# Evicting and scattering an expert's down product behind the branch for long lists, in a mixture-of-experts stage on one core

## The chip, the cores and the metric

One core of a Trainium2 chip runs the whole program: TensorE (PE; its weight loads are shown as PEld), VectorE (DVE), ScalarE (ACT), GpSimd (POOL) and SyncE (SP), with 16 DMA engines. The metric is the device time of one execution in microseconds (us); a smaller time is better.

## The reference

Two blocks follow each other on 512 tokens of width 1024, in float32. The first is a state-space and convolution mixer with an MLP, the second a Fourier and gated-delta mixer followed by the mixture of experts that this case is about:

```python
def moe_ffn(h, w_group, b_group, w_router, b_router, w_gate, w_up, w_down):
    """Hierarchical MoE: top-1 expert group, then top-2 SwiGLU experts within that group."""
...
    def expert_block(args):
        xb, e = args
        hid = jax.nn.silu(xb @ w_gate[e]) * (xb @ w_up[e])
        return hid @ w_down[e]

    ys = lax.map(expert_block, (xs, blk_expert)).reshape(n_slots, d)
    out = jnp.zeros((n + 1, d), ys.dtype).at[slot_tok].add(ys * slot_w[:, None].astype(ys.dtype))
...
    x = x + mod_x[5] * moe_ffn(modulate(rmsnorm_2(x, norm2_g), mod_x[3], mod_x[4]), ...)
...
    return rmsnorm_2(x, final_g)
```

There are 32 experts (4 groups of 8). `w_gate` and `w_up` of one expert are 1024 x 512, `w_down` is 512 x 1024: 6 MB of float32 for each expert. Each token goes to two experts, so 1024 rows are spread over 32 lists whose lengths depend on the data.

## The kernel before, in words

The stage is the function `moe`. It takes the experts one after another, 32 iterations `i`, in 16 pairs `p` (`h` is 0 for the first of a pair, 1 for the second). The first 64 tokens of each list are always computed; what a list holds beyond that is computed behind branches whose condition `nx` (the list's extra blocks of 32 tokens) is read from memory into a register of each engine.

- **Weights.** `load(i)` issues six transfers of 1 MB on SP's queue (L1652) into a ring of 15 chunks. A chunk's next transfer waits until PE has read the chunk for the last time. The up and gate chunks of expert i are read by `gate_up` and by the branch of iteration i, the down chunks in iteration i+1.
- **One iteration on PE**, whose order is written out by hand (`tc.manual_schedule` for PE alone; the order on the other engines is chosen by a planner): `gate_up` (L1733, 32 instructions, in its middle `hide`, the transposes of the previous expert's hidden rows, L1748, copied out by ACT in L1751); for h = 1 `columns` (L1719, 1722), the next pair's tokens turned over; then `finish(i - 1)`, the down product of the previous expert into the PSUM tile `dn` (L1760, 16 instructions); then the branch `longer(i)` (L1900); then small one-hot products (`per_slot`, L1669), for h = 1 after the transposes of `prepare` (L1814).
- **Evict and scatter.** `finish` also holds the eviction of the product by DVE (L1764, in `outputs`), into one of two buffers `y`, and its scatter by POOL to the rows of `yd` in memory (L1703): two rows for each token, one for each of its experts. Both stand ahead of the branch. For the last pair (p = 15) there is no scatter: the rows are split into two parts (L1774, L1775) and placed by one-hot products at the very end (`combined`, L1786, L1787).
- **The branch.** `tc.If(nx > 0, label=...)` at L1900 is entered for a list over 64, an inner `tc.If(nx > 1)` at L1901 for one over 96. A list with one extra block runs `block_up` (L1829) and `block_down` (L1847) in the inner `Else`; a longer one runs `block_up`, `wide_up`, `block_down` and `wide_down` in the inner `If`. `block_down` scatters its product. `wide_down` does not: it splits it and adds it to the accumulator `acc` in SBUF with eight one-hot products (L1786) and eight DVE additions (L1787). The tile `dn` (one buffer) holds the down product of `finish` and also the products of `block_up` and `block_down`.
- **The hint.** In `gate_up` PE is told after its first matmul where the outer branch will jump (`mark_branch_hint_location`). There is no hint for the inner branch, nor on another engine.
- **The end.** In iteration 31 `fetch_back` reads `yd` back in four transfers (L1947), `read_back` adds them to `acc` (L1952, eight DVE additions of 128 x 1024). Two of the four tiles are added with high priority ahead of a branch over all engines (`tc.If(some > 0)`, L2021), the other two at the end. Then come the last expert's product, the one-hot products of the last pair, a norm and the output.

Of the kernel before, what the change touches and what calls it, by code (L numbers as in the profile page):

```python
# [84 lines left out]
class Kern:  # L85
# [1526 lines left out]
    def moe(self, out):  # L1612
# [15 lines left out]
        def t_(tag, shape, dt=F32, bufs=1, pool=mp):  # L1628
            return pool.tile(shape, dt, tag=tag, bufs=bufs, name=self.nm(tag))

        def p_(tag, bufs):
            return pp.tile([P, 512], F32, tag=tag, bufs=bufs, name=self.nm(tag))
# [118 lines left out]
                put(hT[:, q:q + 2], pt[:, 64 * q:64 * q + 128].rearrange("p (k s) -> p k s", k=2))  # L1751
            return hT

        def outputs(ws, hT, wsl):


            dn = p_("dn", 1)
            for q in range(4):
                for j in range(2):
                    M.matmul(dn[64 * j:64 * j + 64], hT[:, q], ws[4 + q // 2][:, q % 2, 512 * j:512 * j + 512],  # L1760
                             start=(q == 0), stop=(q == 3), tile_position=(0, 64 * j), skip_group_check=True)
            self.turn = 4 - self.turn
            y = r1[:, self.turn]
            V.scalar_tensor_tensor(y, dn, wsl, m5, op0=ALU.mult, op1=ALU.mult)  # L1764
            return y

        def down(ws, hT, wsl, idf, yy, tag=""):


            y = outputs(ws, hT, wsl)  # L1770
# [49 lines left out]
            V.tensor_tensor(xb, xb, self.gs[:, 1].unsqueeze(2).broadcast_to(S_), op=ALU.add)  # L1820
            return xb

        def block_up(ws, xb, h):

            gu = p_("dn", 1)
            for k in range(8):
                for o in range(4):
                    j, c = divmod(o, 2)
                    M.matmul(gu[32 * o:32 * o + 32, :256], xb[:, k, 32 * h:32 * h + 32],  # L1829
                             ws[2 * (k // 4) + j][:, k % 4, 256 * c:256 * c + 256],  # L1830
                             start=(k == 0), stop=(k == 7), tile_position=(0, 32 * o), skip_group_check=True)
            sb, hb = (t_(n, [P, 256])[:64] for n in ("sb", "hb"))
            A.activation(sb, gu[64:, :256], AF.Silu)
            V.tensor_mul(hb, gu[:64, :256], sb)
            return hb

        def block_down(ws, w, hb, h, sx):

            pt = p_("tr", 1)
            for c in range(2):  # L1840
                M.transpose(pt[:, c * 64:c * 64 + 64], hb[:, c * P:c * P + P], self.ident[:64, :64])
            hT = t_("hTb", [P, 4, 32])
            V.tensor_copy(hT.rearrange("p (c h) s -> p h c s", h=2), pt[:, :P].rearrange("p (h c s) -> p h c s", h=2, c=2))
            dn = p_("dn", 1)
            for q in range(4):
                for o in range(4):
                    M.matmul(dn[32 * o:32 * o + 32, :256], hT[:, q], ws[4 + q // 2][:, q % 2, 256 * o:256 * o + 256],  # L1847
                             start=(q == 0), stop=(q == 3), tile_position=(0, 32 * o), skip_group_check=True)
            yb = t_("sb", [P, 256])
            V.scalar_tensor_tensor(yb, dn[:, :256], w[:, 1:2], m5b, op0=ALU.mult, op1=ALU.mult)  # L1850
            if sx is not None:
                scatter(sx, yb, 4)
                return
            yH = t_("hb", [P, 256], F32R)
            A.copy(yH, yb)
# [29 lines left out]
        def wide_up(ws):  # L1885
            return gate_up(ws, normed(prepare(64), t_("xb2", [P, 512]).rearrange("p (k s) -> p k s", k=8)), 0, None, "cb", 3)

        def wide_down(ws, w, gh):
            for fn in combined([down(ws, hidden(gh), w[:, 1:2], w[:, 0:1], yx, "b")]):
                fn()  # L1890

        def length(i, **kw):
# [1 line left out]
            return nc.values_load(self.extra[0:1, e:e + 1], min_val=0, max_val=14, **kw)  # L1894

        def longer(i, ws, nx, first, xb, far, label=None):
            w, sx = first[0], first[2]
            if sx is not None:
                sx = sx[:, i % 2:i % 2 + 1]
            with tc.If(nx > 0, label=label):  # L1900
                with tc.If(nx > 1) as more_:  # L1901
                    hb = block_up(ws, xb, i % 2)
                    g = wide_up(ws)
                    block_down(ws, w[:, i % 2], hb, i % 2, sx)
                    wide_down(ws, far[1][:, i % 2], g)
                    with ExitStack() as ies:
                        for b in range(1, INLINE):
                            ies.enter_context(tc.If(nx > 1 + 2 * b))
                            far = further(per_slot(places(ranks(i // 2), 96 + 64 * b, 64, "b"), vals(i // 2)))
                            rows2(far, i % 2)  # L1910
                            wide_down(ws, far[1][:, i % 2], wide_up(ws))
                with more_.Else():
                    block_down(ws, w[:, i % 2], block_up(ws, xb, i % 2), i % 2, sx)

        engs = [mybir.EngineType.PE, mybir.EngineType.DVE, mybir.EngineType.Activation, mybir.EngineType.Pool]
        mes = ExitStack()
# [59 lines left out]

            held["hT"] = hidden(gh, A.copy)

        def finish(i, ws):

            p, h = divmod(i, 2)
            w, sx = wv[p]
            if p < 15:
                scatter(sx[:, h:h + 1], outputs(ws, held["hT"], w[:, h, 1:2]), 2)
            else:
                pair.append(down(ws, held["hT"], w[:, h, 1:2], w[:, h, 0:1], yr[:, h]))

        before = None
        for i in range(32):
            p, h = divmod(i, 2)  # L1990
            if h == 0 and p < 14:
                oh = onehot(p + 2)
            ws = load(i)
            if i == 31:
                for t in range(3):
                    fetch_back(t)
                with tc.high_priority():
                    for t in range(2):
                        read_back(t)
            if h == 0 and 0 < p < 15:  # L2000
                oh1 = places(ranks(p + 1), 64, 32, "1")
            if i:
                with tc.If(length(i, engines=[mybir.EngineType.Pool]) > 1):
                    rows2(far, h)
            if h and p < 15:
                oh2 = places(ranks(p + 1), 96, 64, "2")
            gate_up(ws, xs, 64 * h, gh, between=[hide] if i else [ahead], start=4 if i else 1, label=f"long{i}")
            if i == 0:
                with tc.If(length(0, engines=[mybir.EngineType.Pool]) > 1):
                    rows2(far, 0)  # L2010
                xb = normed(prepare(0), xb1)
                oh1 = places(ranks(1), 64, 32, "1")
            if h and p < 15:
                columns()
            if i:
                finish(i - 1, before)
            nx0, nx = nx, length(i + 1, engines=engs) if i < 31 else None
            if i < 31:
                longer(i, ws, nx0, firsts[p], xb, far, f"long{i}")
            else:  # L2020
                with tc.If(some > 0, label="long31"):  # L2021
                    longer(i, ws, nx0, firsts[p], xb, far)
                    with tc.If(most > 1 + 2 * INLINE):
                        longest()
                fetch_back(3)
            if h and p < 15:
                ps = prepare(0)
                if p < 14:
                    wv.append(fetch(per_slot(oh, vals(p + 2))))
                xb = normed(ps, xb1)  # L2030
                far = further(per_slot(oh2, vals(p + 1)))
            if h == 0 and p < 15:
                firsts.append(more(p + 1, per_slot(oh1, vals(p + 1))))
            if i == 29:
# [5 lines left out]
        finish(31, before)  # L2040
        ob = t_("oh2", [P, T], F32R)
        V.tensor_scalar(ob, iota, firsts[15][1], None, op0=ALU.is_equal)
        pair.append((ob, yyb))
        for t in range(2, 4):
            read_back(t)
        mes.close()

# [67 lines left out]
```

## Time and profile before

| | |
|---|---|
| three runs: median, lowest to highest | 2015.5 us, 2010.29 to 2017.15 us |
| the profiled execution: its own time, its span | 2006.19 us, 2004.4 us |
| mean granted clock of TensorE in it | 0.929 of full speed |
| busy share of the span: PE, DVE, ACT, POOL | 88%, 56%, 29%, 16% |
| expert stage: first gate_up matmul, last product out of it | 1428.8 us, 1983 us |

The span runs from the first to the last instruction; positions in the rows below are us from its start. In this execution four lists are over 64 tokens and one of them is over 96: L1829 ran 256 times, which is 4 times 64, and `gate_up` into `cb` (the wide one) once. Engine names with a q (DVEq, PEq) mean the engine's sequencer, which here is where a branch is passed and signalled.

### The profile page before, as it was taken

To read this page: it belongs to the slowest core of one execution; us is meant where nothing else is said; L and a number is where in the kernel's file an instruction comes from. 1 tells how busy PE (TensorE), PEld (TensorE's weight loads), DVE (VectorE), ACT (ScalarE), POOL (GpSimd) and SP (SyncE) were. 2 spreads that over 40 slices of the span, in tenths; PEclk is the share of its full clock that TensorE was granted. 3 is DMA by queue.
4 is the path that set the end of the run, shared out by engine and by line. 5 is a ranking of instruction groups with operands and counts; after the bars stand their busy time and mean duration, and the time that the engine had idled before them with its cause. 6 is when DMAs were issued, how large, how long until landed. Compare 5 with 4: busy or idle time off the path is not lost. (4 is left out here: it accounts for less than half of the span.)

```text
span 2004.4 us, 24512 instructions
## 1 busy us (share of the span) xinstructions
PE 1767.2 (88%) x9177; PEld 1149.3 (57%) x9177; DVE 1118.7 (56%) x2240; ACT 586.8 (29%) x991; POOL 318.5 (16%) x209
## 2 busy tenths in 40 slices
PE   6778889699999999999988988999598888888984
PEld 4545556376786787777765666887333333333331
DVE  4799898833543665584457698573532223233225
ACT  3122323232433254332335533332411111111112
POOL 0334444421000000000012122003011111101010
PEclk9878889799999999999998898999699989989998
DMA  5111111138556332221222111015799999979994
GB/s 141 57 63 42 45 61 64 42 133 293 184 183 238 106 117 94 85 84 64 84 84 81 47 43 56 12 54 207 290 365 413 412 364 387 367 280 374 415 412 164
DMA packets 150196, 351.07 MB, mean 175 GB/s; under 512 B 20407, under 2 KB 107008, under 8 KB 130155
## 3 DMA queue, kind: packets, MB, share of 16 engines
q1 hardware_dynamic: 135533, 302.52, 40.9%
q0 software_dynamic: 8928, 33.37, 4.6%
q10 hardware_dynamic: 5534, 12.54, 1.7%
q8 instruction: 121, 1.98, 0.4%
q14 instruction: 80, 0.66, 0.1%
HBM read 339.63 MB, written 18.89 MB: 179 GB/s over the span
## 5 line engine op out<-in xcount | busy, mean ns | idle before, releaser
L125 ACT CAST wh<-w 128x1024 fp32r<-128x1024 f32 (+1 forms) x184 | 179.4, 975 | 407.2 <-PE acc L131 339.8
L126 POOL TENSOR_TENSOR wl<-w,wh 128x1024 fp32r<-128x1024 f32 (+1 forms) x76 | 182.8, 2409 | 623.5 <-PE acc L138 372.7
L1733 PE MATMUL gu<-ew,moe 128*64 128x512 f32 x1024 | 259.0, 640 | 9.5 <-issue 5.7
L126 DVE TENSOR_TENSOR wl<-w,wh 128x1024 fp32r<-128x1024 f32 (+1 forms) x108 | 123.2, 1141 | 119.2 <-PE acc L138 88.6
L1733 PEld LDWEIGHTS gu<-ew,moe 128*64 128x64 f32 x1024 | 75.6, 145 | 139.5 <-issue 128.9
L130 PE MATMUL acc<-xH,wh 128*128 128x512 f32 x352 | 152.1, 432 | 0.0
L131 PE MATMUL acc<-xL,wh 128*128 128x512 f32 x352 | 148.7, 422 | 0.0
L1742 DVE TENSOR_TENSOR moe<-gu,moe 64x512 f32<-64x512 f32 x32 | 21.9, 683 | 208.6 <-ACT moe L1741 148.4
L1760 PE MATMUL dn<-ew,hT 128*64 128x512 f32 x528 | 121.9, 604 | 0.4 <-DVE hT L1751 0.4
L130 PE MATMUL acc<-fH,wh 128*128 128x512 f32 x256 | 104.3, 408 | 0.4 <-ACT fH L152 0.4
L130 PE MATMUL acc<-gH,wh 128*128 128x512 f32 x256 | 103.2, 403 | 0.0
L131 PE MATMUL acc<-fL,wh 128*128 128x512 f32 x256 | 102.6, 401 | 0.0
L131 PE MATMUL acc<-gL,wh 128*128 128x512 f32 x256 | 101.9, 398 | 0.0
L1751 ACT COPY hT<-tr 128x128 f32<-128x128 f32 x64 | 13.9, 269 | 300.4 <-PE tr L1748 300.4
L138 PE MATMUL acc<-xH,wl 128*128 128x512 f32 x352 | 94.3, 412 | 6.9 <-DVE wl L126 4.1
L130 PEld LDWEIGHTS acc<-xH,wh 128*128 128x128 f32 x352 | 72.2, 205 | 42.3 <-issue 19.6
L1703 POOL DMA_INDIRECT yd<-moe,sx x30 | 30.0, 999 | 379.4 <-DVEq L1900 341.2
L131 PEld LDWEIGHTS acc<-xL,wh 128*128 128x128 f32 x352 | 72.2, 205 | 21.5 <-issue 5.9
L138 PEld LDWEIGHTS acc<-xH,wl 128*128 128x128 f32 x352 | 68.7, 196 | 24.3 <-DVE wl L126 4.6
L1760 PEld LDWEIGHTS dn<-ew,hT 128*64 128x64 f32 x528 | 36.9, 139 | 70.8 <-issue 64.7
L1764 DVE SCALAR_TENSOR_TENSOR moe<-dn,wv,moe 128x512 f32<-128x512 f32 x33 | 24.8, 750 | 87.5 <-PE dn L1760 87.5
L130 PE MATMUL acc<-hxH,wh 128*128 128x512 f32 x160 | 71.0, 448 | 2.1 <-DVE y L1248 2.1
(708 smaller groups left out, 3465.5 us busy)
## 6 DMA issues: line engine op xcount, KB each, us to landing
ew<-in_w_up_dram SPq DMA_DIRECT2D x64, 1024.0 KB
ew<-in_w_gate_dram SPq DMA_DIRECT2D x64, 1024.0 KB
ew<-in_w_down_dram SPq DMA_DIRECT2D x64, 1024.0 KB
w<-in_w_in_dram SPq DMA_DIRECT2D x36, 1024.0 KB
w<-in_w_ff_dram SPq DMA_DIRECT2D x32, 1024.0 KB
wm<-in_w_mod_dram POOLq DMA_DIRECT2D x24, 1024.0 KB, 6.7
xt<-in_x_dram SPq DMA_DIRECT2D x8, 512.0 KB
w<-in_w_conv_out_dram SPq DMA_DIRECT2D x4, 1024.0 KB
```

The source lines that it names most:

```text
L125: nc.scalar.copy(H[:, :kt], W[:, :kt, c:c + P])
L126: self.lsub.tensor_sub(L[:, :kt], W[:, :kt, c:c + P], f(H[:, :kt]))
L130: self.nc.tensor.matmul(ps, H[:, k], aH[:, k, sl], start=(k == 0), stop=False)
L131: self.nc.tensor.matmul(ps, H[:, k], aL[:, k, sl], start=False, stop=False)
L138: nc.tensor.matmul(ps, L[:, k], aH[:, k, sl], start=False, stop=(k == kt - 1))
L1703: nc.gpsimd.indirect_dma_start(out=self.yd.rearrange("r (m c) -> (r m) c", m=m), out_offset=bass.IndirectOffsetOnAxis(ap=sx, axis=0), in_= ...
L1733: mm = M.matmul(gu[64 * j:64 * j + 64], xs[:, k, s0:s0 + 64], ws[2 * (k // 4) + j][:, k % 4], start=(n == 0), stop=(n == 7), tile_position ...
L1742: V.tensor_mul(gh[:64], gu[:64], gh[64:])
L1751: put(hT[:, q:q + 2], pt[:, 64 * q:64 * q + 128].rearrange("p (k s) -> p k s", k=2))
L1760: M.matmul(dn[64 * j:64 * j + 64], hT[:, q], ws[4 + q // 2][:, q % 2, 512 * j:512 * j + 512], start=(q == 0), stop=(q == 3), tile_position ...
L1764: V.scalar_tensor_tensor(y, dn, wsl, m5, op0=ALU.mult, op1=ALU.mult)
```

## The change

The down product is cut in two. `product` (PE only) stays ahead of the branch, called from a new `begin`; the eviction and the scatter (or, for the last pair, the split) move behind the branch, in `finish`. `block_up` and `block_down` take PSUM tiles from the three buffers of `cb` in place of `dn`, which now stays occupied across the branch. For the pairs with a scatter, `block_up` moves ahead of the inner branch, which gets a label and a hint on PE after block_up's first four matmuls, and `wide_down` scatters its rows to `yd` in place of the split, the one-hot products and the additions; for that it makes its own target rows (`targets`). All four tiles are read back at the very end, without priority.

```diff
-        def outputs(ws, hT, wsl):
-
-
-            dn = p_("dn", 1)
+        def product(ws, hT, dn):
+
             for q in range(4):
                 for j in range(2):
                     M.matmul(dn[64 * j:64 * j + 64], hT[:, q], ws[4 + q // 2][:, q % 2, 512 * j:512 * j + 512],
                              start=(q == 0), stop=(q == 3), tile_position=(0, 64 * j), skip_group_check=True)
+            return dn
+
+        def outputs(dn, wsl):
+
             self.turn = 4 - self.turn
             y = r1[:, self.turn]
             V.scalar_tensor_tensor(y, dn, wsl, m5, op0=ALU.mult, op1=ALU.mult)
             return y
...
-        def block_up(ws, xb, h):
-
-            gu = p_("dn", 1)
+        def block_up(ws, xb, h, label=None):
+
+            gu = p_("cb", 3)
...
+                if k == 0 and label:
+                    with tc.issue_after(mm.ins):
+                        tc.mark_branch_hint_location(label, engines=[mybir.EngineType.PE])
...
-            dn = p_("dn", 1)
+            dn = p_("cb", 3)
...
-        def wide_down(ws, w, gh):
-            for fn in combined([down(ws, hidden(gh), w[:, 1:2], w[:, 0:1], yx, "b")]):
+        def wide_down(ws, w, gh, sx=None):
+            hT = hidden(gh)
+            dn = p_("cb", 3)
+            product(ws, hT, dn)
+            if sx is not None:
+                scatter(sx, outputs(dn, w[:, 1:2]), 2)
+                return
+            for fn in combined([down(dn, w[:, 1:2], w[:, 0:1], yx, "b")]):
                 fn()
...
             with tc.If(nx > 0, label=label):
-                with tc.If(nx > 1) as more_:
-                    hb = block_up(ws, xb, i % 2)
+                if sx is not None:
+                    hb = block_up(ws, xb, h, f"wide{i}")
+                with tc.If(nx > 1, label=f"wide{i}") as more_:
+                    if sx is None:
+                        hb = block_up(ws, xb, h)
+                    s2 = wide(far)
                     g = wide_up(ws)
-                    block_down(ws, w[:, i % 2], hb, i % 2, sx)
-                    wide_down(ws, far[1][:, i % 2], g)
+                    block_down(ws, w[:, h], hb, h, sx)
+                    wide_down(ws, far[1][:, h], g, s2)
...
                 with more_.Else():
-                    block_down(ws, w[:, i % 2], block_up(ws, xb, i % 2), i % 2, sx)
+                    if sx is None:
+                        hb = block_up(ws, xb, h)
+                    block_down(ws, w[:, h], hb, h, sx)
...
-        def finish(i, ws):
-
+        def begin(ws):
+
+            held["dn"] = p_("dn", 1)
+            product(ws, held["hT"], held["dn"])
+
+        def finish(i):
             p, h = divmod(i, 2)
             w, sx = wv[p]
             if p < 15:
-                scatter(sx[:, h:h + 1], outputs(ws, held["hT"], w[:, h, 1:2]), 2)
+                scatter(sx[:, h:h + 1], outputs(held["dn"], w[:, h, 1:2]), 2)
...
                     fetch_back(t)
-                with tc.high_priority():
-                    for t in range(2):
-                        read_back(t)
...
             if i:
-                finish(i - 1, before)
+                begin(before)
             nx0, nx = nx, length(i + 1, engines=engs) if i < 31 else None
             if i < 31:
                 longer(i, ws, nx0, firsts[p], xb, far, f"long{i}")
...
                 fetch_back(3)
+            if i:
+                finish(i - 1)
...
-        for t in range(2, 4):
+        for t in range(4):
             read_back(t)
```

## Rows read from the trace of the kernel before

**Rows 1.** Windows of the expert stage: length, busy us (instructions) PE PEld DVE ACT POOL, clock, DMA, GB/s.
```profile
1461.00:1600.00 139.00, 121.33 (x596) 48.93 (x596) 41.99 (x155) 20.85 (x59) 16.38 (x16) 0.94 1.02 410
1600.00:1740.00 140.00, 122.74 (x796) 52.96 (x796) 40.23 (x144) 20.97 (x59) 17.56 (x18) 0.96 0.97 381
1740.00:1765.00 25.00, 18.82 (x100) 7.89 (x102) 10.90 (x24) 1.82 (x3) 1.00 (x1) 0.90 0.46 179
1765.00:1847.00 82.00, 73.32 (x422) 29.41 (x418) 22.09 (x81) 14.22 (x40) 8.02 (x8) 0.95 0.93 369
1847.00:1957.00 110.00, 96.70 (x474) 37.36 (x472) 30.23 (x106) 15.89 (x45) 11.40 (x11) 0.97 1.01 405
```
**Rows 2.** Waits of PE from 1428 to 1847 us: us in total, times, longest.
```profile
PE cb L1669 <- DVEq L1900: 10.3, 8, 2.3
PE xt L1814 <- DVEq L1900: 9.7, 8, 1.3
PE dn L1829 <- issue: 7.8, 3, 2.6
PE xt L1814 <- PEq L1900: 6.7, 3, 3.7
```
**Rows 3.** Timeline around the branch of iteration 12: start, us, instruction, idle before.
```profile
1639.52 0.68 DVE L1742 TENSOR_TENSOR moe<-gu,moe 64x512 f32<-64x512 f32 x1 [11.50 <-ACTq L1900]
...
1642.27 0.75 DVE L1764 SCALAR_TENSOR_TENSOR moe<-dn,wv,moe 128x512 f32<-128x512 f32 x1 [2.07 <-PE dn L1760]
...
1643.34 0.58 PE L1669 MATMUL cb<-vals,oh 128*128 128x6 f32 x4 [1.12 <-DVEq L1900]
```
**Rows 4.** Timeline behind the branch of iteration 30, where no one-hot product follows.
```profile
1950.61 1.83 PE L1733 MATMUL gu<-ew,moe 128*64 128x512 f32 x4 [0.31 <-PEq L1900]
```
**Rows 5.** DVE's sequencer at the two branch lines: ns min/median/max, first and last start.
```profile
L1900 DVEq COMPARE_BRANCH  x31: 50/56/72, 1444.9 to 1950.7; - x31
...
L1900 DVEq EVENT_SEMAPHORE  x27: 21/21/21, 1445.2 to 1951.1; - x27
...
L2021 DVEq EVENT_SEMAPHORE  x2: 21/21/21, 1976.0 to 1976.1; - x2
...
L2021 DVEq COMPARE_BRANCH  x1: 56/56/56, 1973.0 to 1973.0; - x1
```
**Rows 6.** Timeline of the end of the one wide list, iteration 18.
```profile
1755.51 0.75 DVE L1764 SCALAR_TENSOR_TENSOR moe<-dn,wv,moe 128x512 f32<-128x512 f32 x1 [3.56 <-PE dn L1760]
...
1763.45 0.99 PE L1669 MATMUL cb<-vals,oh 128*128 128x6 f32 x4 [1.15 <-DVEq L1906]
```
**Rows 7.** Windows of single gate_up runs and iterations, L1733 alone: length, PE, PEld, clock, DMA, GB/s.
```profile
1764.37:1774.84 10.47, 10.15 (x32) 2.78 (x32) 0.72 0.93 384
1835.30:1842.93 7.63, 7.31 (x32) 2.12 (x32) 1.00 1.02 408
...
1535.08:1556.73 21.65, 7.46 (x32) 2.97 (x33) 0.88 1.02 415
1507.29:1522.39 15.10, 7.31 (x33) 2.12 (x33) 1.00 1.02 412
```
**Rows 8.** POOL's sequencer waits in the scatters: ns min/median/max, first and last start.
```profile
L1703 POOLq EVENT_SEMAPHORE  x62: 17/42/7648, 1453.3 to 1941.2; - x62
```
**Rows 9.** Timeline of the end, DVE and PE.
```profile
1964.00 0.68 DVE L1742 TENSOR_TENSOR moe<-gu,moe 64x512 f32<-64x512 f32 x1 [12.90 <-ACT moe L1741]
...
1976.19 0.66 PE L1748 MATMUL tr<-pk,moe 64*128 64x64 f32 x4 [9.49 <-DVEq L2021]
...
1990.86 0.69 DVE L1787 TENSOR_TENSOR x<-x,cb 128x512 f32<-128x512 f32 x1
```
**Rows 10.** DVE's groups from 1950 us to the end: count, busy us, mean ns.
```profile
L1952 DVE TENSOR_TENSOR x<-x,yd 128x1024 f32<-128x1024 f32 x8 | 9.6, 1222 | 2.7 <-DVEq L2021 2.6
L1787 DVE TENSOR_TENSOR x<-x,cb 128x512 f32<-128x512 f32 x8 | 5.2, 684 | 0.1
...
L1775 DVE TENSOR_TENSOR moey<-moe,moey 64x512 fp32r<-64x512 f32 x4 | 2.7, 686 | 0.8 <-ACT moey L1774 0.7
```

More of the change, by code (lines that the diff above doesn't have):

```diff
@@ L1765, in outputs, with down @@
             return y
-        def down(ws, hT, wsl, idf, yy, tag=""):
-            y = outputs(ws, hT, wsl)
+        def down(dn, wsl, idf, yy, tag=""):
+            y = outputs(dn, wsl)
             for j in range(2):
@@ L1828, in block_up @@
                     j, c = divmod(o, 2)
-                    M.matmul(gu[32 * o:32 * o + 32, :256], xb[:, k, 32 * h:32 * h + 32],
-                             ws[2 * (k // 4) + j][:, k % 4, 256 * c:256 * c + 256],
+                    mm = M.matmul(gu[32 * o:32 * o + 32, :256], xb[:, k, 32 * h:32 * h + 32],
+                                  ws[2 * (k // 4) + j][:, k % 4, 256 * c:256 * c + 256],
                              start=(k == 0), stop=(k == 7), tile_position=(0, 32 * o), skip_group_check=True)
+                if k == 0 and label:
+                    with tc.issue_after(mm.ins):
+                        tc.mark_branch_hint_location(label, engines=[mybir.EngineType.PE])
             sb, hb = (t_(n, [P, 256])[:64] for n in ("sb", "hb"))
@@ L1896, in longer, with wide @@
         def longer(i, ws, nx, first, xb, far, label=None):
+            h = i % 2
             w, sx = first[0], first[2]
             if sx is not None:
-                sx = sx[:, i % 2:i % 2 + 1]
+                sx = sx[:, h:h + 1]
+            def wide(far):
+                return targets(far[1], 64, "2")[:, h:h + 1] if sx is not None else None
             with tc.If(nx > 0, label=label):
-                with tc.If(nx > 1) as more_:
-                    hb = block_up(ws, xb, i % 2)
+                if sx is not None:
[4 more added lines that the diff above has]
+                    s2 = wide(far)
                     g = wide_up(ws)
-                    block_down(ws, w[:, i % 2], hb, i % 2, sx)
-                    wide_down(ws, far[1][:, i % 2], g)
+                    block_down(ws, w[:, h], hb, h, sx)
+                    wide_down(ws, far[1][:, h], g, s2)
                     with ExitStack() as ies:
@@ L1909, in longer @@
                             far = further(per_slot(places(ranks(i // 2), 96 + 64 * b, 64, "b"), vals(i // 2)))
-                            rows2(far, i % 2)
-                            wide_down(ws, far[1][:, i % 2], wide_up(ws))
+                            rows2(far, h)
+                            s2 = wide(far)
+                            wide_down(ws, far[1][:, h], wide_up(ws), s2)
                 with more_.Else():
-                    block_down(ws, w[:, i % 2], block_up(ws, xb, i % 2), i % 2, sx)
+                    if sx is None:
+                        hb = block_up(ws, xb, h)
+                    block_down(ws, w[:, h], hb, h, sx)
         engs = [mybir.EngineType.PE, mybir.EngineType.DVE, mybir.EngineType.Activation, mybir.EngineType.Pool]
@@ L1983, in finish @@
             if p < 15:
-                scatter(sx[:, h:h + 1], outputs(ws, held["hT"], w[:, h, 1:2]), 2)
+                scatter(sx[:, h:h + 1], outputs(held["dn"], w[:, h, 1:2]), 2)
             else:
-                pair.append(down(ws, held["hT"], w[:, h, 1:2], w[:, h, 0:1], yr[:, h]))
+                pair.append(down(held["dn"], w[:, h, 1:2], w[:, h, 0:1], yr[:, h]))
         before = None
@@ L2039, in moe @@
         hide()
-        finish(31, before)
+        begin(before)
+        finish(31)
         ob = t_("oh2", [P, T], F32R)
```

## The prediction, before the run

> **What bounds the kernel now.** The windows of the expert stage come first [rows 1]. The reader is to see two things. From 1461 to 1600 us and again from 1847 to 1957 us the DMA engines are busy without a break (share 1.01 to 1.02, 410 and 405 GB/s); between them the share sinks to 0.97, 0.46 and 0.93. There the ring of 15 chunks is full and SP waits for PE to free one. So PE sets the pace between 1600 and 1847 us, and transfers nearly do before and after. The waits of PE come second [rows 2]: up to 1847 us no weight stands among its largest waits. What stands there is DVE's passing of the branch line L1900 (10.3 us in 8 waits and 9.7 us in 8), three stalls on the way into block_up (7.8 us) and three slow jumps of PE itself (6.7 us). Third, the timeline at one branch shows why DVE is late [rows 3]: it finished the activation product at 1640.20 us (1639.52 + 0.68) and then stands before its eviction, which needs the down product that PE ends at 1642.2. The eviction ends at 1643.02, then DVE passes the branch and signals, and PE goes on at 1643.34, 1.12 us after its last matmul. Last, the end [rows 9]: PE stands 9.49 us for DVE's passing of L2021.
>
> **Part 1: eviction and scatter behind the branch.** No instruction is added; DVE's 0.75 us and POOL's scatter only change places with the branch. DVE now reaches the branch after the activation product, at 1640.2 in the example, 2.0 us before PE does. What remains of PE's wait is bounded below by the 0.31 us of the one iteration where PE's next work waits for its own jump alone [rows 4] and above by what it is now. I take 0.31, because DVE is early by more than the price of its own passing: in its last pass of L1900, 1950.7 to 1951.1, it took 0.4 us [rows 5]. Up to 1847 us the waits are 20.0 us in 16; the longest, 2.3, is that of iteration 0, which has no eviction, so 17.7 us in 15 remain, and 17.7 - 15 x 0.31 = 13.0 us are won on PE.
>
> At the other branch, L2021, DVE needed 3.0 us, 1973.0 to 1976.0 [rows 5]. The Trainium skill ("Runtime: NRT & Kernel Launch", section "Instruction fetch mechanics") says that a taken branch to a target outside the instructions fetched in sequence stops the engine until a DMA has brought them. By that rule every skip of the long body would cost DVE what L2021 costs; the 0.4 us at L1900 speaks against it for that line. Its price is worked out from rows among the rivals.
>
> What is queued behind the moved work: on DVE the list indices of the next pair, which wait for PE's one-hot products anyway; on POOL the gathers. A scatter can wait up to 7.65 us for an earlier one to land [rows 8]. Behind a taken branch the moved scatter now stands behind the branch's own, so POOL may be held that long four or five times. PE meets it only if the next eviction were held too, a whole iteration later (13 to 15 us [rows 7]). I cost it at nothing; with that cover gone it is 7.65 us a time.
>
> **Part 2: lists with one extra block** (three up to 1847 us). PE stands 2.5 to 2.6 us at the jump into block_up, 7.8 us together [rows 2], at no other engine's work ("issue"). With block_up ahead of the inner branch PE falls straight into it, on a PSUM tile that nobody must empty first, and the jump passes under block_up's own matmuls. I take the 0.31 of rows 4 for what remains: 7.8 - 3 x 0.31 = 6.9 us; the other bound is nothing, if the jump shows up behind block_up.
>
> **Part 3: the wide list** (one). From its eviction's start, 1755.51, to PE's next work, 1763.45, PE spent 7.9 us on eviction, split, eight products and eight additions [rows 6]. Now only the eviction and the signal may stand there, 1.0 us by rows 3 (0.75 and some 0.3). That wins 6.9 us, or 7.6 if PE needn't wait for it. The added target rows are two tiny DVE operations under PE's transposes: nothing. The idling had one more price: the next gate_up ran at a granted clock of 0.72, 10.47 us against 7.63 us at 1.00 [rows 7]. With PE going on, 2.8 us more are won (below: 0, above: 2.8).
>
> PE wins 13.0 + 6.9 + 6.9 + 2.8 = 29.6 us up to 1847 us.
>
> **What the transfers give back.** The last run, 1847 to 1957, has no room: the DMA engines are busy all the time, and the seven branch waits that PE saves there only make it wait for weights. Its end moves by as much as its beginning moves. How far can that go? Against 410 GB/s the three windows with pauses hold 29/410 x 140 = 9.9, 231/410 x 25 = 14.1 and 41/410 x 82 = 8.2, together 32 us of time without transfers. The 29.6 us fit, but barely, and some of them are won in the first window, which has no pauses: about half of the 15 waits, 7 us, can only eat up the lead of the ring there. I let half of that, 3.5 us, come back as waits, and 1 us more in the others: 25 us. Ends: 16.6 us if all 13.0 of the waits come back, 29.6 if none do.
>
> **Part 4: the end.** Between the product and L2021 DVE did an eviction, its split and four read-back additions. Now it reaches that branch at 1964.68 (1964.00 + 0.68 [rows 9]), passes it in 3.0 us [rows 5], and PE goes on at about 1968 instead of 1976.19: 8 us. But the work only moves behind the branch. From there DVE has 2 x 0.75 (evictions [rows 3]) + 2.7 + 9.6 + 5.2 [rows 10] and three one-hot compares, at most 0.68 each like the 128 x 512 additions: 21.0 us. Never idle, it would end at 1989.0, against 1991.55 before (1990.86 + 0.69): 2.5 us is the most. If the planner puts all eight read-backs behind the last eviction, DVE idles while PE makes the last product, some 5 us, and 2.5 us are lost. Before, the planner slid read-backs into that hole, so I expect it to do so again, with a little idling: 1.3 us won.
>
> **The sum.** 25 + 1.3 = 26.3 us off the profiled execution's own time of 2006.2: 1979.9 us. That execution lies 0.5% under the median of the three runs, so the same share, 1.3%, off 2015.5 gives 1989 us.
>
> **The rivals.**
> - *Weights take it back.* With PE faster by 0.9 us per iteration the transfers bind sooner, and the branch waits return as waits for chunks. For it: 1.02 in the first window, 0.93 and 0.97 later. Against: three lists and the wide one refill the ring. 16.6 + 1.3 = 18 us: 1997 us.
> - *The branch wait stays in half of the iterations.* If DVE's jump at L1900 costs 3.0 us once no eviction covers it, DVE passes at 1640.2 + 3.0 = 1643.2, and PE starts as late as it does now; where columns stand before the product DVE is earlier and no loss arises. The cb waits (10.3 - 2.3 - 7 x 0.31 = 5.8 us) are kept. Against: the 0.4 us. 26.3 - 5.8 = 20.5 us: 1995 us. This is also what the rule of the Trainium skill in "Runtime: NRT & Kernel Launch", "Instruction fetch mechanics", would make of it.
> - *Hidden anyway.* If the ring's lead, not PE, decides in the middle too, as the shares of 0.97 and 0.93 allow, only the pause of the wide list shrinks, by some 5 us: 2010 us.
> - *Slower: jumps of PE that miss.* Three times PE itself was late at L1900 (6.7 us, longest 3.7 [rows 2]), and the clock fell behind it: that iteration took 21.65 us against 15.10 [rows 7], 6.6 us. The change moves every branch target on PE. Four more such misses eat the gain, from five on it is slower; six give 2006.2 + 13.3, as a median 2029 us. For it: the misses exist and nothing in the rows says why these iterations have them. Against: the hint stays where it was and PE's branch bodies get shorter.
>
> **How the numbers follow.** The forecast has 0.50, its own range 1981 to 1997; weights take it back 0.17; the wait stays 0.12; hidden anyway 0.10; missing jumps 0.09; a gain over 35 us (no misses at all, nothing given back) 0.02. A measurement of this kernel can tell about 0.3%, 6 us, from no change. Faster: 0.50 + 0.17 + 0.12 + 0.02 and a fifth of the hidden case, 0.83. Same: the rest of it, 0.08. Slower: 0.09. The range leaves out the missing jumps, part of the hidden case and the largest gains: 1976 to 2010.
>
> **What would show it.** Right: PE's waits for DVEq L1900 fall to a few us in total, with 0.3 us at most branches; no stall before block_up; 6 to 8 us less between the wide product and PE's next work and no fallen clock behind it; DMA share near 1 from 1600 us on; more waits for ew chunks near the end; PE's wait at L2021 near 2 us, the last addition at most 2.5 us sooner after the penultimate product. Wrong: waits named PEq L1900 of 3 us in many iterations, waits of 1.1 us named DVEq or ACTq as now, or POOL holding evictions.

## The result, and the profile after

The changed kernel takes 1985.97 us (median of 6 runs, 1983.46 to 1997.39) against 2015.01 us for the kernel before on the same chip: a ratio of 0.9874, interval 0.9835 to 0.9913. The medians lie 29 us apart; the ratio, which goes by the means of the runs, makes it 25 us. Timed again on another chip it took 1990.01 us against 2010.76, ratio 0.9901 (0.9874 to 0.9929), 20 us. The forecast was 1989 us, a ratio of 0.987, in a range of 1976 to 2010.

The profiled execution took 1987.15 us, span 1985.4 us. From the first gate_up to the end of the down product of expert 30 it is 520.58 us (1427.62 to 1948.20), where the kernel before needed 537.93 (1428.77 to 1966.70): 17.35 us less. This stretch is called the stage below. From there to the end it is 37.15 us, where it was 37.70. So the gain lies in the stage, as forecast, and hardly at the end. The two profiled executions differ by 19.0 us, less than the medians: the one of the kernel before took 2006.19 us, 9 under its median.

The windows of the stage, after; columns as in [rows 1]:

```profile
1460.00:1600.00 140.00, 124.83 (x638) 48.02 (x634) 40.07 (x145) 21.20 (x60) 13.12 (x13) 0.95 1.02 413
1600.00:1740.00 140.00, 126.65 (x762) 51.40 (x762) 40.88 (x146) 20.55 (x58) 17.98 (x17) 0.96 0.99 394
1740.00:1765.00 25.00, 22.71 (x146) 10.12 (x146) 9.21 (x32) 4.52 (x12) 4.72 (x5) 1.00 0.68 247
1765.00:1847.00 82.00, 76.50 (x446) 29.84 (x442) 25.54 (x95) 11.74 (x34) 10.28 (x10) 0.96 1.02 411
```

The three windows that had pauses in the transfers, 0.97, 0.46 and 0.93 in [rows 1], now show 0.99, 0.68 and 1.02. What is left of the pauses lies around the wide list.

The waits of PE over the whole stage, after:

```profile
PE xt L1816 <- PEq L1917: 15.8, 15, 3.7
PE gu L1733 <- DMA ew<-in_w_gate_dram: 8.7, 7, 1.6
...
PE cb L1669 <- issue: 4.8, 3, 1.7
PE gu L1733 <- DMA ew<-in_w_up_dram: 4.7, 3, 2.4
...
PE cb L1669 <- PEq L1917: 3.1, 10, 0.3
PE cb L1669 <- DVEq L1917: 2.3, 1, 2.3
```

L1917 is the branch that was L1900. DVE's passing of it, the head of the list in [rows 2], is left once, in iteration 0, which has no eviction. In its place PE waits for its own jump alone: 0.3 us in the even iterations, 0.4 in most odd ones, and 3.6 to 3.7 us in three (9, 17 and 25); such a long wait of PE for its own jump is called a late jump below. New are 13.4 us of waits for weight chunks, where before 3.0 us in 2 stood in the whole stage, and three stalls of 1.4 to 1.75 us in iterations 7, 15 and 23, for which the profile names no other engine ("issue").

PE's timeline behind a list of one block (iteration 10) and at the branch of iteration 11:

```profile
1594.60 3.66 PE L1831 MATMUL cb<-ew,xb 128*32 128x256 f32 x64
...
1602.80 0.58 PE L1669 MATMUL cb<-vals,oh 128*128 128x6 f32 x4 [0.70 <-DVE sb L1855]
...
1615.96 0.68 PE L1816 MATMUL xt<-pk,moe 64*128 64x64 f32 x8 [0.41 <-PEq L1917]
```

No idle time stands before block_up any more; 2.6 us stood there [rows 2]. Behind the block PE waits 0.70 us for its eviction.

The end of the wide list, after:

```profile
1743.59 3.65 PE L1758 MATMUL cb<-ew,hT 128*64 128x512 f32 x16 [0.50 <-DVE hT L1751]
1748.23 0.58 PE L1669 MATMUL cb<-vals,oh 128*128 128x6 f32 x4 [0.99 <-DVEq L1927]
1748.74 3.65 PE L1733 MATMUL gu<-ew,moe 128*64 128x512 f32 x16
```

The product ends at 1747.24, PE goes on 0.99 us later (forecast 1.0, before 7.9 with the eviction [rows 6]), and sixteen gate_up matmuls take 3.65 us, those of full clock: the fall to 0.72 [rows 7] is gone.

The end, PE and then DVE:

```profile
1944.60 3.60 PE L1758 MATMUL dn<-ew,hT 128*64 128x512 f32 x16
1950.43 0.56 PE L1748 MATMUL tr<-pk,moe 64*128 64x64 f32 x4 [2.23 <-DVEq L2046]
1951.51 6.55 PE L1758 MATMUL dn<-ew,hT 128*64 128x512 f32 x16 [0.52 <-ACT hT L1751]
```

```profile
1950.66 0.75 DVE L1766 SCALAR_TENSOR_TENSOR moe<-dn,wv,moe 128x512 f32<-128x512 f32 x1 [4.48 <-DVEq L2046]
...
1958.10 0.75 DVE L1766 SCALAR_TENSOR_TENSOR moe<-dn,wv,moe 128x512 f32<-128x512 f32 x1 [1.74 <-PE dn L1758]
...
1971.74 0.69 DVE L1789 TENSOR_TENSOR x<-x,cb 128x512 f32<-128x512 f32 x1
```

PE's 9.49 us at the last branch [rows 9] are 2.23, and yet DVE's last addition ends 24.2 us behind the product (1972.43 - 1948.20) where it was 24.85 (1991.55 - 1966.70). DVE idles 4.48 us at the branch and 1.74 us for the last product. The last product, begun behind PE's stall, ran 6.55 us (5.75 before) where the one ahead of the stall took 3.60.

### The profile page after: what moved, and what is told of

It is laid out like the page before. It is cut to its first block, busy times and chain, and to the rows that moved or that the text cites. A ratio compares the mean times of both kernels' runs of the same rounds, so it can differ in the third digit from the quotient of the medians.

```text
span 1985.4 us, 24482 instructions
## 1 busy us (share of the span) xinstructions
PE 1765.2 (89%) x9169; PEld 1143.1 (58%) x9169; DVE 1114.9 (56%) x2231; ACT 585.3 (29%) x989; POOL 321.8 (16%) x210
## 5 line engine op out<-in xcount | busy, mean ns | idle before, releaser
L1733 PE MATMUL gu<-ew,moe 128*64 128x512 f32 x1024 | 262.5, 639 | 14.2 <-DMA ew<-in_w_gate_dram 8.7
L1733 PEld LDWEIGHTS gu<-ew,moe 128*64 128x64 f32 x1024 | 73.9, 145 | 147.8 <-issue 120.4
```

Of the source, the lines that this page charges most:

```text
L1733: mm = M.matmul(gu[64 * j:64 * j + 64], xs[:, k, s0:s0 + 64], ws[2 * (k // 4) + j][:, k % 4], start=(n == 0), stop=(n == 7), tile_position ...
```

## The experiments

**The parts one by one.** First the eviction and scatter behind the branch alone: against the whole change, the lists and the reading back are as before.

```diff
-                return targets(far[1], 64, "2")[:, h:h + 1] if sx is not None else None
+                return None
...
-                if sx is not None:
-                    hb = block_up(ws, xb, h, f"wide{i}")
-                with tc.If(nx > 1, label=f"wide{i}") as more_:
-                    if sx is None:
-                        hb = block_up(ws, xb, h)
+                with tc.If(nx > 1) as more_:
+                    hb = block_up(ws, xb, h)
```

> The change's first part alone: eviction and scatter behind the branch (block products in cb), but block_up inside both inner branches without a hint, the wide list with split, one-hot products and additions, two tiles read back ahead of the last branch as before. Theory (PE sets the pace, and transfers give back what they can't deliver): PE's gap at branches not entered falls from 1.1 to 0.3 or 0.4 us, the 2.5 us stall before block_up stays, the expert stage (first gate_up matmul to the end of the down product of expert 30) shrinks from 537.9 by 9 to 13 us; time 9 to 13 us less. Rival (the lists make the gain, the branch wait returns as waits for weights at once): stage shorter by less than 5 us.

Measured: 2002.22 us against 2012.3, ratio 0.9948 (0.9929 to 0.9967), 10 us less. Its waits of PE in the stage:

```profile
PE gu L1733 <- DMA ew<-in_w_gate_dram: 12.9, 9, 2.4
PE gu L1733 <- DMA ew<-in_w_up_dram: 7.6, 5, 2.4
PE cb L1831 <- issue: 7.3, 2, 4.9
PE xt L1816 <- PEq L1917: 6.3, 15, 0.5
```

The branch waits are gone here too, and 20.5 us of waits for weights stand in their place. The stall before block_up, which was expected to stay, stands in one list of three only, there with 7.3 us in two pieces. The stage of this profiled execution is 537.50 us, 0.4 less than before, which is the rival's sign; but the two profiled executions differ by no more than that as a whole (2005.75 against 2006.19 us), since this one lies over its median and that of the kernel before under its own. So the time of all runs decides: about 10 us, where the forecast's Part 1 with its own give-back had 13.0 - 3.5 = 9.5.

Then the lists alone (block_up hoisted and hinted, `wide_down` scattering), with `finish(i - 1)` called right behind `begin` as before, and the reading back as before.

```diff
                 begin(before)
+                finish(i - 1)
...
-            if i:
-                finish(i - 1)
```

> The list parts alone: block_up ahead of the inner branch with its hint, the wide list scatters; eviction and scatter of the down product stay ahead of the branch, two tiles read back early as before. Theory: PE's waits for DVEq at the branch stay at about 20 us up to the last wide list and after it, the stall before block_up (7.8 us) goes, the wide list ends 7 us sooner and the clock stays up behind it: stage shorter by 12 to 16 us, time likewise. With the first part alone at 9 to 13 the two add up to more than the 17.4 us that the whole change takes off the stage, since the transfers take some back when both are there. Rival (no giving back, each term was simply smaller): stage shorter by 5 to 8 us, the two adding up to 17.

Measured: 1992.35 us, ratio 0.9900 (0.988 to 0.9919), 20 us less, more than expected. Its waits of PE:

```profile
PE xt L1816 <- DVEq L1917: 13.2, 11, 1.3
PE xt L1816 <- PEq L1917: 12.2, 4, 3.5
PE cb L1669 <- DVEq L1917: 11.8, 10, 2.3
```

DVE's branch waits stay at 25.0 us, and still the whole gain is there as far as these runs can tell: the stage is 520.81 us, that of the whole change 520.58, and the ratio lies with the two of the whole change, 0.9874 and 0.9901. By their ratios the two parts add up to 30 us (0.52% and 1.00%); the whole gave 25 and 20 in its two timings: they overlap. Moving the eviction wins 10 us by itself, but on top of the lists no run shows that it wins anything.

Third, the reading back alone, in the kernel before:

```diff
-                with tc.high_priority():
-                    for t in range(2):
-                        read_back(t)
...
-        for t in range(2, 4):
+        for t in range(4):
             read_back(t)
```

> The kernel before with one edit: all four tiles read back at the very end, none early. Theory: DVE passes the last branch about 4.9 us sooner (four additions of 1.22 us fewer ahead of it), PE's wait there falls from 9.5 to about 4.6 us, but the additions are done later: the end moves by no more than 2 us either way; the stage before is untouched. Rival (the late read-back makes the gain at the end): 4 to 5 us less.

Measured: ratio 1.0015 (0.9996 to 1.0034), no change. PE's wait at the last branch is 8.5 us instead of 9.49, not the 4.6 expected. DVE does reach that branch sooner, 3.3 us behind the product (1972.16 to 1975.5) instead of 6.3, but then it needs 5.0 us to pass it, where [rows 5] had 3.0:

```profile
1980.76 4.63 DVE L1952 TENSOR_TENSOR x<-x,yd 128x1024 f32<-128x1024 f32 x4 [5.70 <-DVEq L2018]
```

**How much PE wins where transfers don't bind.** In both kernels the down weights of expert 0 serve all experts, so that a third of the weight transfers is left out; the ring then holds 3.25 experts' chunks (13 / 4) instead of 2.5 (15 / 6). These two are called lightened.

```diff
+                if w is wd and i:
+                    ts.append(downs[k0 // 2])
+                    continue
```

> The kernel before with a third of the expert transfers left out: the down weights of expert 0 are loaded once and serve all 32 experts, the ring keeps 13 chunks for up and gate weights. The output is therefore that of other weights; only the time is read. 4 MB per expert need 10.6 us at 395 GB/s for SP's queue, less than any iteration takes on PE, so PE alone sets the pace. Theory: stage within 6 us of the 537.9 us of the kernel before, whose transfers hardly bound it; no waits for ew at the end.

> The changed kernel with the same third of the transfers left out (down weights of expert 0 serve all, output that of other weights). Theory (transfers took back 10 to 14 us of what PE won): stage shorter than in the light kernel before by 28 to 36 us, no waits for ew, DMA share well under 1. Rival (PE itself won only what the stage shows, 17 us, and the transfers took nothing): shorter by 15 to 20 us, as with all weights.

Measured: 1981.85 us against 2008.9 for the lightened kernel before (ratio 0.9846, 0.9813 to 0.9879), and 1943.51 us for the lightened changed one (0.9663, 0.9633 to 0.9693). The first expectation fell: the transfers already cost the kernel before 27 us, with no more than 3.0 us of waits for chunks to show for it. What the lightening takes away there are above all stalls of PE itself. In the stage before stand

```profile
PE xt L1814 <- PEq L1900: 9.8, 4, 3.7
PE gu L1733 <- issue: 5.7, 3, 3.1
```

and the 7.8 us on the way into block_up [rows 2], 23.3 us together. In the lightened kernel before all three are gone, and block_up (L1837 there) waits for the eviction alone:

```profile
PE dn L1837 <- DVE moe L1772: 4.2, 4, 1.4
```

So these stalls came with the transfers here. The second expectation held in kind and was exceeded: the change is worth 38.3 us there, and 41.9 us in the profiled stage, for 28 to 36.

The whole stage in one window each, in the order of before, after, lightened before (with its iterations 6 and 8) and lightened after (with its iteration 6); columns as in [rows 1]:

```profile
1428.77:1966.70 537.93, 471.28 (x2540) 190.94 (x2540) 157.09 (x555) 83.28 (x233) 55.44 (x54) 0.94 0.95 376
```

```profile
1427.62:1948.20 520.58, 469.75 (x2532) 185.91 (x2532) 152.30 (x546) 81.94 (x231) 57.16 (x55) 0.95 0.97 390
```

```profile
1432.12:1943.39 511.27, 463.57 (x2540) 185.52 (x2540) 157.79 (x556) 83.29 (x233) 54.41 (x54) 0.95 0.69 267
1523.31:1537.70 14.39, 13.27 (x58) 4.52 (x57) 4.64 (x16) 1.03 (x3) 1.68 (x2) 0.88 0.77 303
1552.64:1565.33 12.69, 11.57 (x58) 4.11 (x57) 4.75 (x16) 1.03 (x3) 1.59 (x2) 1.00 0.92 356
```

```profile
1434.73:1904.11 469.38, 443.09 (x2532) 177.18 (x2532) 152.19 (x546) 82.08 (x231) 56.48 (x55) 0.98 0.75 292
1517.17:1529.05 11.88, 11.57 (x57) 4.11 (x56) 5.18 (x16) 1.03 (x3) 1.11 (x2) 1.00 0.93 377
```

The first number behind the length is PE's busy time, the rest of the length its idle time. With light transfers the change cuts the idle time by 21.4 us (47.70 to 26.29) and the busy time by 20.5. Of the latter 3.95 us are the eight products of the wide list that are gone (their busy time in the window of 1756.3 to 1763.4 us of the kernel before); the other 16.5 us are the same matmuls in a shorter time, at a higher granted clock, 0.98 against 0.95. The short windows show one case: iteration 6 of the lightened kernel before has the same work as its iteration 8, but at a clock of 0.88, and PE is busy 1.7 us longer; after the change that iteration has 1.00 and 11.88 us.

With all transfers the change cuts the idle time by 15.8 us (66.65 to 50.83), but the busy time only by 1.5, which is less than those eight products. So of the 24.5 us that the transfers take back in the stage (41.9 - 17.35), 5.6 are idle time and 18.9 are the same matmuls taking longer.

These sizes belong to four single executions, and two of those lie off their medians: the kernel before at 2006.19 us, under it, and the lightened kernel before at 1987.37, the slowest of its six, with a granted clock of 0.930 where the six have 0.934 on average. A second pair of traces with the same code in the stage, the third experiment's and the unedited changed kernel's further down, makes it 15.6 us of matmuls instead of 18.9 (20.48 - 4.87):

```profile
1431.01:1972.16 541.15, 473.39 (x2540) 191.41 (x2540) 157.29 (x555) 83.27 (x233) 55.42 (x54) 0.93 0.94 372
```

```profile
1429.65:1950.43 520.78, 468.52 (x2532) 184.74 (x2532) 151.98 (x546) 81.93 (x231) 56.36 (x55) 0.95 0.97 389
```

The granted clock is known of every timed execution. Taking (1 - clock) x span as an estimate of what the clock costs a whole execution, the means are 143 to 146 us for the kernel before (three series), 135 and 138 after, 130 and 117 lightened before and after. By that the change wins some 8 us of clock with all transfers and some 14 with light ones, and the transfers take back about 6 us as clock, with a standard error of about 4. So some give-back as clock is likely, and 18.9 us is its upper end.

PE's timeline of iterations 6 and 7 of the changed kernel shows where such time arises:

```profile
1515.22 2.79 PE L1733 MATMUL gu<-ew,moe 128*64 128x512 f32 x10 [1.04 <-DMA ew<-in_w_gate_dram]
...
1528.98 1.07 PE L1733 MATMUL gu<-ew,moe 128*64 128x512 f32 x2 [1.38 <-DMA ew<-in_w_up_dram]
1531.64 5.38 PE L1733 MATMUL gu<-ew,moe 128*64 128x512 f32 x10 [1.59 <-DMA ew<-in_w_gate_dram]
...
1537.57 3.65 PE L1733 MATMUL gu<-ew,moe 128*64 128x512 f32 x16
```

Behind two waits for chunks in iteration 7, 2.97 us, ten matmuls take 5.38 us, where the same ten took 2.79 us behind the single wait of iteration 6: the stall costs 2.6 us more than its length. Around those ten matmuls the granted clock is at the lower of its two levels, 1.2 in place of 2.4 GHz (0.52 in the window). Not every such stall does this: in the first experiment's trace ten matmuls behind two waits of 1.58 and 1.74 us took 2.79 us. The window of iteration 7:

```profile
1530.50:1537.00 6.50, 5.36 (x11) 1.28 (x11) 0.00 (x0) 0.00 (x0) 0.00 (x0) 0.52 1.04 417
```

**The wide list as before, in the changed kernel.**

```diff
-                return targets(far[1], 64, "2")[:, h:h + 1] if sx is not None else None
+                return None
```

> The changed kernel, but the wide list is split and added by one-hot products as before, in place of the scatter. Theory: some 7 us between the wide list's down product and PE's next work come back, the clock falls behind them, and since nothing hides them from PE the stage is 7 to 10 us longer than in the changed kernel. Rival (transfers decide there already): less than 3 us longer.

Measured: 2000.3 us, ratio 0.9956 (0.9937 to 0.9975), 14 us above the changed kernel's first median and 10 above its second (on other chips), which is what was expected or somewhat more. The waits for chunks are twice those of the changed kernel, 26.7 us, though its transfers have more time:

```profile
PE gu L1733 <- DMA ew<-in_w_gate_dram: 13.8, 10, 2.3
PE gu L1733 <- DMA ew<-in_w_up_dram: 12.9, 7, 2.4
```

A reading of this, not shown: while PE stands at the wide list with the ring full, no transfer starts, and that pause comes back later as waits for weights. It fits the windows after (the DMA share around 1740 rose from 0.46 to 0.68); the runs don't separate it from the clock's part.

**A hint for the last branch.** In the changed kernel DVE and ACT get a hint for that branch in iteration 31.

```diff
+            if i == 31:
+                tc.mark_branch_hint_location("long31", engines=[mybir.EngineType.DVE, mybir.EngineType.Activation])
```

> The changed kernel with one addition: in the last iteration DVE and ACT get the branch hint for the last branch too. Theory (DVE's passing of that branch, 3 us in both traces, is a late fetch of its target): DVE passes in under 1 us, PE's wait there falls from 2.2 us to 0.3, the end comes 1.5 to 2.5 us sooner. Rival (the 3 us are something else, or another engine is next): PE's wait stays at 2 us or more.

Measured: 1989.75 us, ratio 0.9897 (0.9858 to 0.9936), by time not told from the change without it. In the profile PE's wait there falls from 2.23 to 0.51 us, and from the product to the end it is 33.11 us instead of 37.15:

```profile
1956.16 0.43 PE L1748 MATMUL tr<-pk,moe 64*128 64x64 f32 x4 [0.51 <-PEq L2048]
1957.00 3.23 PE L1758 MATMUL dn<-ew,hT 128*64 128x512 f32 x14 [0.40 <-ACT hT L1751]
```

DVE's own passing, from its compare to its signal, falls from 3.6 us (1946.7 to 1950.3) to 0.6:

```profile
L2048 DVEq EVENT_SEMAPHORE  x2: 21/21/21, 1954.7 to 1954.8; - x2
...
L2048 DVEq COMPARE_BRANCH  x1: 79/79/79, 1954.1 to 1954.1; - x1
```

So the 3 us of [rows 5] are a price that a hint ahead of time takes away, as it would a late fetch of the target, and with the stall went the slow clock of the last product. The Trainium skill ("Runtime: NRT & Kernel Launch", section "Instruction fetch mechanics") has the rule: a taken branch to a target outside the instructions fetched in sequence stops its engine until a DMA has brought them. The traces agree at this branch. At L1917 DVE passes without such a stop (0.5 us from its last compare to its last signal) and PE waits for its own jump; whether DVE's target there lies outside what was fetched, no run shows.

**The late jumps of PE.** Three variants and the changed kernel again, on one chip. The hint for the outer branch comes half a gate_up later:

```diff
-                if n == 0 and label:
+                if n == 4 and label:
```

The inner hint is left out, with block_up still ahead of the branch:

```diff
-                    hb = block_up(ws, xb, h, f"wide{i}")
+                    hb = block_up(ws, xb, h)
```

The third has the later hint and the hint for the last branch together.

> The whole change, unedited, timed beside the three variants that follow on one chip. Theory (the net gain is about 1.3%, 20 to 30 us): a ratio of 0.985 to 0.990 to the kernel before. It is the reference that the next two are read against; a spread of the late passages of TensorE through its outer branch in another profiled execution (three of 3.6 to 3.7 us in the first, at iterations 9, 17 and 25) tells whether they belong to those iterations.

> The whole change, with TensorE's hint for the outer branch issued behind the third quarter's start of gate_up (n = 4) instead of behind its first pair of matmuls, so about half as far ahead of the branch. Theory A (the late passages are hints whose fetch was lost or overtaken because it came early): the three passages of 3.6 to 3.7 us at iterations 9, 17 and 25 go, up to 11 us of TensorE's time, and the kernel gains 5 to 10 us on the unedited one (ratio between the two 0.995 to 0.9975). Theory B (a fetch that competes with the weights' transfers is late whenever it is asked for): the late passages stay as many or become more, the time stays within 4 us or grows, since the hint has less lead.

> The whole change without the hint for the inner branch; the first block's gate and up still stand ahead of that branch. Theory (the hint hides the fetch): in the iterations that have a list TensorE passes the inner branch late, 2 to 4 us in each of four to five iterations, 8 to 15 us in all, and the kernel is that much slower than the unedited one. Rival (standing ahead of the branch, the first block's 32 matmuls already cover the fetch): no wait of more than 1 us at that branch, time within 4 us of the unedited one.

> The whole change with the outer hint later (as the run with the moved hint) and the hint for VectorE and ScalarE ahead of the last branch. Theory: the two are in different stages and add, so the end's 4 us of the tail and whatever the moved hint brings, 4 to 12 us under the unedited kernel. Rival: the transfers set the stage, the moved hint brings nothing, and what is left is 0 to 4 us.

Measured: 1990.01 us unedited (0.9901), 1994.72 with the later hint (0.9925, 0.9902 to 0.9949), 1992.78 without the inner hint (0.9907, 0.9878 to 0.9937) and 1991.42 with both hints (0.9907, 0.988 to 0.9934). The later hint doesn't remove the late jumps: six of 1.9 to 3.7 us against five of 2.0 to 3.7 in the unedited one. Iterations 9, 17 and 25 are late in all of them. The waits of PE with the later hint:

```profile
PE xt L1816 <- PEq L1917: 14.2, 15, 3.7
```

Theory A falls: the hint's distance isn't the cause. Two other things go with them. One is the load: the lightened kernel before has no late jump and the lightened changed one two, of 1.7 and 2.0 us. The other is the kernel: the kernel before is late in iterations 7, 11, 19 and 27, the changed kernel with the wide list as before in none, and every full-weight variant with the new wide list in 9, 17 and 25. The code of the branch alone doesn't settle it: the third experiment, edited at the end only, is late in 7, 11, 24, 25 and 27. Iterations 9, 17 and 25 are eight apart, and so are 7, 15 and 23 with the stalls named "issue"; the runs don't say what recurs there. PE's compare and branch at that line in the changed kernel, ns min/median/max (4460 at most when lightened):

```profile
L1917 PEldq COMPARE_BRANCH  x31: 74/436/6185, 1437.9 to 1925.0; - x31
```

Without the inner hint PE's timeline of iteration 10 is the same as with it; in iteration 14 it stalls inside block_down:

```profile
1606.47 0.30 PE L1846 MATMUL tr<-pk,hb 64*128 64x64 f32 x2 [1.15 <-DVE hb L1839]
...
1671.56 3.42 PE L1852 MATMUL cb<-ew,hTb 128*32 128x256 f32 x30 [2.17 <-issue]
```

With the hint such a stall stands in iteration 10 of the unedited kernel here, behind block_up:

```profile
1600.18 0.31 PE L1846 MATMUL tr<-pk,hb 64*128 64x64 f32 x2 [3.00 <-issue]
```

So with the hoist no list has a stall before block_up, with the hint or without it, and the hint is worth nothing that these runs can tell; but in single lists a stall of 2 to 3 us now stands further on. The two hints together are 3.3 us under the later hint alone (intervals overlap), near the 3.7 us by which the last stretch is shorter (33.32 against 37.02 us).

## Why the prediction was right

The net was right, and each wait moved the way that was forecast. But PE's own gain and what the transfers take back were both forecast too small, and that the two errors nearly cancel is luck. The parts also don't add up as the sum had them.

- *Part 1.* Right: 15 waits fell to 0.3 and 0.4 us. DVE passed L1917 early, so the rival that the wait stays in half of the iterations is out, and with it what the rule of the Trainium skill, applied to that branch, would have given. The moved eviction had to wait for a scatter to land three times (6.8 us in all), and PE never for it: nothing, as costed. As a term of the sum it failed: alone it gives 10 us, but the lists without it do as well as the whole.
- *Part 2.* Right in kind: the 7.8 us of stalls before block_up are gone. In most lists the jump did pass under block_up; the other bound, that it shows up behind, came true in iteration 10 of the second profile (3.00 us). Waits of 0.70 us for the block's eviction, 2.1 us in all, follow it. The lightened kernel before lacks these stalls too, so they were not the jump's price alone.
- *Part 3.* Idle time and products as forecast (0.99 us against 1.0). The 2.8 us of clock came too, but the clock is the term that was mis-sized: the forecast counted one fall. With light transfers the change takes 16.5 us of slow matmuls out of the profiled stage, some 14 us by the clocks of all executions; iteration 6 above shows one behind a plain branch wait of 1.25 us, while iteration 8, behind one of 1.11, lost nothing.
- *What the transfers give back.* This is the step that failed in size. The forecast let 4.5 us of PE's 29.6 come back, as waits. In timed runs it is 38.3 us won with light transfers and 25 or 20 with all (1.26% and 0.99%), thus 13 to 18 given back. In the profiled stages it is 41.9 won and 24.5 given back, 5.6 of it idle time and the rest slower matmuls; by the clocks of all executions only about 6 us of it are clock, so how the give-back divides stays open. The pair isn't quite PE's own gain either, since the lightened kernel before already lacks 23.3 us of stalls, Part 2's among them. The bound of the forecast, 32 us of time without transfers, wasn't reached: at 390 GB/s on average against 413 in the fullest window, some 29 us of the 520.58 are still without transfers (520.58 x 23/413). That PE and the transfers now wait for each other by turns is a reading, not shown. (The last run held six branch waits, not the seven of the forecast; no term used that number.)
- *Part 4.* Right in its sign: 0.6 us won for a forecast of 1.3, DVE's work only moved; the planner slid read-backs between the evictions, as assumed. DVE passed the last branch in 3.6 us where 3.0 were forecast, and the last product at a low clock, 6.55 us for 5.75, took 0.8.
- *The rivals.* Weights take it back is half true: waits for chunks rose to 13.4 us, and the 19.0 us between the two profiled executions are nearer its 18 than the forecast's 26; the two timings, 25 and 20 us by their ratios, lie between. The slower case is out: late jumps number three, in the second profile five, against four before (five in the third experiment). They did move to other iterations. Hidden anyway is out.

Open remains what makes iterations 9, 17 and 25 late whatever the hint does, how much of the give-back is clock, and why the moved eviction adds nothing to the lists that these runs can tell.

## What to carry to other kernels

Before counting waits on an engine that is nearly bound by transfers, count what each wait does to the clock behind it: here, with light transfers, the change won 14 to 16.5 us of clock beside 21.4 us of waits, and some of it came back with the transfers' stalls. A wait at a branch can be moved cheaply, by putting work that the others needn't wait for behind the branch; here that won 10 us alone and nothing measurable beside the lists, so time each part without the other. To know what transfers take back, lighten them in both kernels; but read what else the lightening takes away, and set single profiled executions against the times and clocks of all runs before a term is sized from them.

## What the runs showed of the hardware

- Two waits in gate_up, 2.97 us together, were followed by ten matmuls that took 5.38 us instead of 2.79. In the lightened changed kernel sixteen matmuls behind a late jump of 1.95 us took 5.35 us instead of 3.65; behind its other late jump, 1.74 us, they took 3.65:

```profile
1740.33 0.68 PE L1824 MATMUL xt<-pk,moe 64*128 64x64 f32 x8 [1.95 <-PEq L1925]
...
1741.92 5.35 PE L1741 MATMUL gu<-ew,moe 128*64 128x512 f32 x16
```

- PE's compare and branch at L1917, with a hint, takes 0.4 us at the median and 6.2 us at most (3.7 us of idle PE), 4.5 us at most when a third of the weight transfers is gone (2.0 us of idle PE).
- With a third of the weight transfers gone, 23.3 us of PE's stalls at jumps and ahead of block_up and gate_up vanished from the stage of the kernel before, of which no wait named a transfer.
- DVE's passing of the last branch, from compare to signal, took 2.8 to 5.9 us in the eleven traces without a hint for it, with light transfers too (3.1 and 5.9), and 0.6 us in the two with one. The hint on DVE and ACT took 1.7 us off PE's wait there and 4.0 us off the last stretch.
